# Neighbourhood probabilities of a two-layer encoder: the exchange of partition quarters as four writes to DRAM and one read back, instead of 16 transfers inside SBUF

## The chip, the cores and the metric

The kernel runs on one core of a Trainium2 chip. Its time is the device time of one execution, in microseconds (us). The core has a matrix engine (TensorE, PE), which reads SBUF and writes PSUM; a vector engine (VectorE, DVE); a scalar engine (ScalarE, ACT); a general engine (GpSimd, POOL); and a queue engine (SyncE, SP), which in this kernel issues the DMA transfers. SBUF has 128 partitions. A transfer is issued by SP and then moves on 16 DMA engines while SP goes on to its next instruction.

## The reference, cut to what matters

Two encoder layers on 512 tokens of width 1024, in float32. Each layer adds a mixer, a cross attention to 256 memory tokens and a convolutional feed-forward to x. Half of the mixer's heads (8 of 64 channels) do neighbourhood attention (NA): the tokens are a grid of 8 rows by 64 columns, and each query sees a window of 8 rows and 16 columns.

```python
scores = jnp.einsum('brqhd,brikhd->bhrqik', q, k_rows) * (dh ** -0.5)
scores = scores + bias[None]
scores = jnp.where(col_valid[None, None, None, :, None, :], scores, NEG_INF)
p = jax.nn.softmax(scores, axis=(-2, -1))
o = jnp.einsum('bhrqik,brikhd->brqhd', p, v_rows)
```

The change concerns p on its way from the softmax to the last product: scores come out with queries on partitions, and the product with V needs keys on partitions.

## The kernel before, in words

Every float32 operand of a matmul is split into a high and a low part, and three matmuls make one product. In the program's names, raw is a weight as it comes from DRAM, hi and lo its parts (made on ACT, L273, and POOL, L274), xg the normalised input, mm and sc tiles in PSUM, r and t tiles in SBUF, and u the tiles of this change: 128 partitions by 2048 elements, 1 MB, from a pool of two buffers.

The NA stage of a layer goes through the heads in four pairs p = 0 to 3, each in two units u = 2p + bp. Per pair:

- Scores (na_scores): eight 128x256 matmuls a unit, queries on partitions. DVE adds the bias and takes the row's bound (L766), ACT takes the exponential (L772). The K tile of a pair is split on ACT (L689) and DVE (L693) for one half of the partitions, and then "doubled": two DMAs copy it to the other half of the partitions (r<-r, 64 partitions, 256 KB each). The scores of the pair wait for that.
- Turn (na_turn): DVE takes the reciprocal of the sums (L782), ACT (L791) and POOL (L495) multiply, and DVE transposes 32x32 blocks into the pair's u tile (L793), eight instructions of 256 elements per unit.
- Exchange (na_exchange, L795 to L804): a block transpose leaves a block in the quarter of partitions (32 of them) in which it was. Sixteen DMAs move each quarter's four parts to the four quarters of a second u tile, 64 KB each, all issued by SP.
- Split (na_split): from that second tile, ACT casts the high part (L822, four instructions), and DVE and POOL subtract for the low part (L823, two each).
- Values (na_values): matmuls with V (mm<-r,r 128x256 on PE); two halves are added on ACT (L842) and DVE (L843, L844).

weave calls these steps, step s of the list working on unit s minus its lag; between them (None) the filler puts matmuls of projections, so that PE has work while a unit is on the other engines:

```python
weave(8, [(2, na_exchange), (3, na_split), None, (1, na_turn), (0, na_scores), None,
          (3, na_values_of), None], attn_fill.run, na_quanta)
```

The instructions of PE and of SP run in the order in which this code issues them. A doubling is issued by a rule of its own (late): its place comes when PE's programmed work has advanced far enough. The instructions of ACT, DVE and POOL are placed by a scheduler from the dependencies and from priorities, before the kernel runs, so a change at one place moves instructions near it. In every engine's program the order is then fixed: an instruction that waits holds up those behind it. An instruction that writes a buffer waits for the readers of what was in it.

Other transfers on SP that stand near the exchange: the weights (raw), the bias of the next pair (r<-in_bias), the memory tokens (r<-in_memT), the rope swaps of the other half of the heads (t<-t, four of 64 KB), a straddling of V (r<-r x5).

Of the kernel before, what the change touches and what calls it, by code (L numbers as in the profile page):

```python
# [10 lines left out]
F32 = mybir.dt.float32  # L11
# [8 lines left out]
S = 512  # L20
# [140 lines left out]
def weave(n, steps, filler, quanta):  # L161


    last = max(st[0] for st in steps if st)
    for s in range(n + last):
        pieces = iter(quanta(s))
        for st in steps:
            if st is None:
                filler(next(pieces))
            elif 0 <= s - st[0] < n:  # L170
                st[1](s - st[0])
# [3 lines left out]
def encoder_kernel(ctx: ExitStack, tc: tile.TileContext, t: dict, out: bass.AP):  # L175
    nc = tc.nc
    PE, SP = Counted(tc, nc.tensor), InOrder(tc, nc.sync)
    late = Late(PE)
    ACT_IN_ORDER = InOrder(tc, nc.scalar)
    ACT, DVE, POOL = Free(nc.scalar), Free(nc.vector), Free(nc.gpsimd)  # L180
# [6 lines left out]
    spool = ctx.enter_context(tc.tile_pool(name="spool", bufs=23))  # L187
    upool = ctx.enter_context(tc.tile_pool(name="upool", bufs=2))
    psum = ctx.enter_context(tc.tile_pool(name="psum", bufs=2, space=PSUM))

    @contextmanager
    def behind(n):
# [9 lines left out]
    def nm(s):  # L202
        uid[0] += 1
        return f"{s}_{uid[0]}"
# [18 lines left out]
    def turned():  # L223
        return upool.tile([P, 4 * S], F32, tag="u", name=nm("u"))
# [146 lines left out]
    for n in FIRST:  # L371
# [3 lines left out]
        u, k0, k1 = n  # L375
# [118 lines left out]
    def normalise(e, sums, col, eng=DVE):  # L494
        eng.tensor_scalar(e, e, sums[:, col : col + 1], 1.0, op0=ALU.mult, op1=ALU.mult)  # L495
# [89 lines left out]
    for n in FIRST:  # L585
# [3 lines left out]
        u, k0, k1 = n  # L589
# [6 lines left out]
        k = slice(k0, k1)  # L596
# [15 lines left out]
    for l in range(DEPTH):  # L612
# [163 lines left out]
        turns, flats = {}, {}  # L776

        def na_turn(u):

            p, bp = divmod(u, 2)  # L780
            es, sums = na.pop(u)
            DVE.reciprocal(sums, sums)  # L782
            if bp == 0:
                turns[p] = turned()
            to = turns[p].rearrange("p (k j b q) -> p j b k q", k=8, j=2, b=4)
            for j in range(2):
                for i in range(2):
                    if i or j:
                        normalise(es[j][:, i, :], sums, 2 * j + i, POOL)
                    else:  # L790
                        ACT.activation(es[j][:, i, :], es[j][:, i, :], AF.Copy, scale=sums[:, 2 * j + i : 2 * j + i + 1])  # L791
                for i in range(2):
                    DVE.transpose(to[:, j, 2 * bp + i], es[j][:, i, :].rearrange("p (k q) -> p k q", q=32))  # L793

        def exchange(src, chunks):  # L795

            dst = turned()
            to = dst.rearrange("p (r c n) -> p r c n", r=4, c=chunks)
            of = src.rearrange("p (c r n) -> p r c n", r=4, c=chunks)
            for d in range(4):  # L800
                for q in range(4):
                    r = (q + d) % 4
                    SP.dma_start(to[32 * r : 32 * r + 32, q], of[32 * q : 32 * q + 32, r])
            return dst  # L804

        def na_exchange(u):
            p, bp = divmod(u, 2)
            if bp == 1:
                flats[p] = exchange(turns.pop(p), 2)

        def na_split(u):
            p, bp = divmod(u, 2)
# [289 lines left out]
        def na_quanta(s):  # L1102
# [4 lines left out]
            if s == 3:  # L1107
# [2 lines left out]
                gqa_eps()  # L1110
            return [NA_FILL] * 3

        weave(8, [(2, na_exchange), (3, na_split), None, (1, na_turn), (0, na_scores), None, (3, na_values_of), None],
              attn_fill.run, na_quanta)
        weave(4 * NB, [(2, gqa_transpose_p), (1, gqa_normalise), (0, gqa_scores), (3, lambda u: gqa_values(u, 0)),
                       (4, lambda u: gqa_values(u, 1)), None], attn_fill.run, lambda s: [GQA_FILL[s]])
# [332 lines left out]
```

## Time and profile before

| | us |
|---|---|
| median of 3 runs | 1415.88 (1415.84 to 1417.39) |
| the profiled execution | 1421.33 |
| its span | 1419.6 |
| NA stage of layer 0 | about 55 to 165 |
| NA stage of layer 1 | about 755 to 865 |

The profile gives busy times of each engine in a stretch, the instructions of an engine in order of time with the idle time before each and what ended it (in square brackets), the waits grouped by what ended them, and the DMA's packets and bytes. A row "sc<-r,r x2 [4.61 <-DMA r<-r]" reads: two matmuls that make scores, before which the engine was idle for 4.61 us, until a DMA from a tile r to a tile r had landed. For SP (SPq) the length of a row is the time in which it issued the DMAs of the row, not the time that they took to land.

### The profile page before, as it was taken

Reading aid. Unit: us, or ns where it says so; the run is one execution under the profiler, and the core shown is the slowest. Engines: PE = TensorE matmul, PEld = TensorE weight load, DVE = VectorE, ACT = ScalarE, POOL = GpSimd, SP = SyncE. Lnnn points to the kernel's source line nnn. Section 1 sums busy time; section 2 is a strip of 40 time slices with the busy share of each in tenths; the row PEclk is TensorE's granted clock in tenths of the full one; section 3 lists DMA queues with packets and bytes.
Section 4 is the critical chain, followed back from the end, with each engine's and each line's share of the span. In section 5 each row is a group of like instructions: output and inputs, shape, how many; then the busy total and the mean of one; then the engine's idle time right before and its main releaser. Section 6 shows DMA issues by size and latency. Waiting matters only on the chain.

```text
span 1419.6 us, 19227 instructions
## 1 busy us (share of the span) xinstructions
PE 1359.4 (96%) x6940; PEld 1156.2 (81%) x6940; DVE 897.2 (63%) x1588; ACT 676.8 (48%) x1258; POOL 713.6 (50%) x509
## 2 busy tenths in 40 slices
PE   9987899999999999999997788999999999999997
PEld 7876789887888888888886777898888888888897
DVE  6667577557587178358546677765658852871874
ACT  6655467555444143234455546774644422342441
POOL 2556656554444444444544477476264444444441
PEclk9997899999999999999998999999999999999998
DMA  6774312231433332333257553123233333333331
GB/s 215 215 190 119 105 31 75 75 104 45 119 89 104 92 101 85 108 90 95 84 178 201 133 134 90 30 88 95 71 90 90 104 92 102 89 91 110 95 91 60
DMA packets 229598, 148.27 MB, mean 104 GB/s; under 512 B 8192, under 2 KB 222464, under 8 KB 229504
## 3 DMA queue, kind: packets, MB, share of 16 engines
q1 hardware_dynamic: 228400, 146.39, 35.6%
q8 instruction: 55, 0.90, 0.3%
q10 hardware_dynamic: 1104, 0.66, 0.1%
q14 instruction: 39, 0.32, 0.1%
HBM read 126.05 MB, written 2.10 MB: 90 GB/s over the span
## 4 chain that ended last, share of the span: by engine, by line
PE 81%; DVE 6%; DMA 4%; ACT 2%; SPq 2%; POOL 2%; issue 2%; ACTq 0%; DVEq 0%; POOLq 0%
PE mm L76 73%; PE sc L76 5%; PE tr L63 2%; SPq L63 2%; PE tr L76 1%; POOL lo L274 1%; DMA r<-in_memT 1%; DMA r<-r 1%; DMA raw<-in_w_in 1%; DVE u L793 1%; DVE r L823 1%; DMA r<-in_rope 1%; DVE r L709 1%; DVE mm L432 1%; ACT hi L273 1%
## 5 line engine op out<-in xcount | busy, mean ns | idle before, releaser
L274 POOL TENSOR_TENSOR lo<-raw,hi 128x1024 fp32r<-128x1024 f32 (+2 forms) x268 | 501.3, 1882 | 459.0 <-ACT hi L273 458.9
L76 PE MATMUL mm<-xg,hi 128*128 128x512 f32 x1920 | 602.3, 395 | 0.9 <-DVE t L844 0.9
L76 PEld LDWEIGHTS mm<-xg,hi 128*128 128x128 f32 x1920 | 362.7, 191 | 74.8 <-ACT t L842 1.1
L273 ACT CAST hi<-raw 128x512 fp32r<-128x512 f32 (+2 forms) x276 | 224.3, 836 | 338.8 <-PE mm L76 275.3
L76 PE MATMUL mm<-xg,lo 128*128 128x512 f32 x960 | 377.5, 393 | 0.0
L76 PE MATMUL mm<-r,hi 128*128 128x512 f32 (+1 forms) x1144 | 331.7, 374 | 1.9 <-DVE xg L446 1.6
L76 PEld LDWEIGHTS mm<-r,hi 128*128 128x128 f32 x1144 | 207.0, 189 | 40.1 <-DVE xg L446 3.2
L1272 DVE SCALAR_TENSOR_TENSOR t<-t,par,t 128x7 f32<-128x7 f32 (+1 forms) x352 | 201.9, 640 | 34.0 <-ACT t L1265 34.0
L76 PEld LDWEIGHTS mm<-xg,lo 128*128 128x128 f32 x960 | 182.9, 191 | 39.1
L76 PE MATMUL mm<-r,lo 128*128 128x512 f32 (+1 forms) x572 | 212.9, 372 | 0.0
L76 PEld LDWEIGHTS mm<-r,lo 128*128 128x128 f32 x572 | 107.8, 188 | 18.9
L495 POOL TENSOR_SCALAR t<-t,s 128x512 f32<-128x512 f32 (+1 forms) x112 | 66.9, 613 | 86.6 <-DVE s L782 43.9
L1257 DVE TENSOR_TENSOR t<-mm,rep 128x512 f32<-128x512 f32 x88 | 60.1, 687 | 77.7 <-PE mm L76 62.1
L76 PE MATMUL sc<-r,r 128*128 128x256 f32 (+1 forms) x352 | 76.7, 350 | 22.3 <-DMA r<-r 17.9
L1278 DVE TENSOR_TENSOR r<-t,r 128x512 fp32r<-128x512 f32 x44 | 90.5, 2057 | 7.4 <-ACT r L1277 4.3
L1274 ACT ACTIVATE t<-t 128x512 f32<-128x512 f32 x44 | 27.9, 633 | 134.8 <-DVE t L1272 134.7
L1301 DVE TENSOR_TENSOR xT<-xT,mm 128x512 f32<-128x512 f32 x32 | 21.9, 685 | 106.8 <-PE mm L76 106.8
L76 PE MATMUL mm<-r,r 128*128 128x256 f32 (+1 forms) x428 | 65.5, 304 | 18.0 <-DVE t L844 8.6
L76 PEld LDWEIGHTS sc<-r,r 128*128 128x128 f32 x352 | 54.7, 203 | 30.4 <-issue 10.4
L76 PEld LDWEIGHTS mm<-r,r 128*128 128x128 f32 x428 | 57.1, 194 | 23.0 <-issue 10.7
L1265 ACT ACTIVATE t<-t,par 128x512 f32<-128x512 f32 x88 | 66.8, 806 | 3.3 <-DVE t L1257 3.3
L959 ACT ACTIVATE t<-sc,s 128x512 f32<-128x512 f32 x64 | 44.1, 691 | 24.5 <-DVE s L957 21.7
(157 smaller groups left out, 1612.1 us busy)
## 6 DMA issues: line engine op xcount, KB each, us to landing
raw<-in_w_up SPq DMA_DIRECT2D x88, 512.0 KB, 3.6
raw<-in_w_in SPq DMA_DIRECT2D x33, 512.0 KB, 4.2
raw<-in_w_down SPq DMA_DIRECT2D x32, 448.0 KB, 3.4
u<-u SPq DMA_DIRECT2D x128, 64.0 KB, 2.0
raw<-in_w_mem_kv SPq DMA_DIRECT2D x16, 512.0 KB, 3.6
raw<-in_w_down SPq DMA_DIRECT2D x16, 512.0 KB, 3.6
r<-in_bias SPq DMA_DIRECT2D x16, 384.0 KB, 6.0
r<-r SPq DMA_DIRECT2D x22, 256.0 KB, 6.0
```

Of the source, the lines that this page charges most:

```text
L63: return lambda *a, **k: self.tc.keep_in_program_order(op(*a, **k))
L76: return self.tc.keep_in_program_order(self.engine.matmul(out, lhsT, rhs, **k))
L273: act.copy(hi[:, k], raw[:, k])
L274: (POOL if eng[0] == "P" else DVE).tensor_sub(lo[:, k], raw[:, k], f(hi)[:, k])
L495: eng.tensor_scalar(e, e, sums[:, col : col + 1], 1.0, op0=ALU.mult, op1=ALU.mult)
L959: ACT.activation(e, sc[j], AF.Exp, bias=nmx[:, c], accum_out=sums[:, c])
L1257: DVE.tensor_mul(u, us[side], ffn.rep)
L1265: ACT.activation(cc, u, AF.Identity, bias=par[:, l, CB + ch : CB + ch + 1], scale=w[1])
L1272: DVE.scalar_tensor_tensor(cc[:, dst], u[:, src], wi, cc[:, dst], op0=ALU.mult, op1=ALU.add)
L1274: ACT.activation(cs[0], cs[0], AF.Silu)
L1278: DVE.tensor_sub(acts[j][1], cs[0], f(acts[j][0]))
L1301: DVE.tensor_add(xT[m], xT[m], pm)
```

## The change

The 16 transfers from quarter to quarter become two steps. Four stores (na_store, one per source quarter, 32 partitions, 256 KB each) write a tile d in DRAM, whose layout puts the target's rows together. One load (na_load, 128 partitions, 1 MB) reads it into the second u tile. The load waits until the four stores have landed. It is a step of its own in the weave's list, ahead of the values and behind the scores, so other transfers can stand between the stores and the load. The transposes write the turned tile in another order (quarter outside, half inside), so that a store reads 2 KB runs; their number and size stay. A pool of two DRAM tiles is new. The lines behind the change move by one, and later by four: L822 and L823 become L826 and L827, L793 becomes L794.

```diff
+    dpool = ctx.enter_context(tc.tile_pool(name="dpool", bufs=2, space=bass.MemoryType.DRAM))
...
-            to = turns[p].rearrange("p (k j b q) -> p j b k q", k=8, j=2, b=4)
+            to = turns[p].rearrange("p (r c j b q) -> p j b c r q", r=4, c=2, j=2, b=4)
...
-                    DVE.transpose(to[:, j, 2 * bp + i], es[j][:, i, :].rearrange("p (k q) -> p k q", q=32))
-
-        def exchange(src, chunks):
-
-            dst = turned()
-            to = dst.rearrange("p (r c n) -> p r c n", r=4, c=chunks)
-            of = src.rearrange("p (c r n) -> p r c n", r=4, c=chunks)
-            for d in range(4):
-                for q in range(4):
-                    r = (q + d) % 4
-                    SP.dma_start(to[32 * r : 32 * r + 32, q], of[32 * q : 32 * q + 32, r])
-            return dst
-
-        def na_exchange(u):
+                    DVE.transpose(to[:, j, 2 * bp + i], es[j][:, i, :].rearrange("p (c r q) -> p c r q", c=2, r=4))
+
+        def store(src):
+
+            d = dpool.tile([4, 32, 4, S], F32, tag="d", name=nm("d"))
+            of = src.rearrange("p (r n) -> p r n", r=4)
+            for q in range(4):
+                SP.dma_start(d[:, :, q].rearrange("r k n -> k r n"), of[32 * q : 32 * q + 32])
+            return d
+
+        def na_store(u):
             p, bp = divmod(u, 2)
             if bp == 1:
-                flats[p] = exchange(turns.pop(p), 2)
+                turns[p] = store(turns.pop(p))
+
+        def na_load(u):
+            p, bp = divmod(u, 2)
+            if bp == 1:
+                flats[p] = turned()
+                SP.dma_start(flats[p], turns.pop(p).rearrange("r k q n -> (r k) (q n)"))
...
-        weave(8, [(2, na_exchange), (3, na_split), None, (1, na_turn), (0, na_scores), None, (3, na_values_of), None],
+        weave(8, [(2, na_store), (3, na_split), None, (1, na_turn), (0, na_scores), None, (2, na_load), (3, na_values_of), None],
```

PE's program is the same instruction for instruction. SP's differs at the eight pairs, and the scheduled engines differ in the two NA stages. Three places follow; a number behind a name tells tiles apart, and the same tile has another number in the two kernels.

The first is SP in layer 0, pair 0, before: the exchange, a weight, and the doubling of the next K tile (r_691, r_692).

```order
L63 DMA r_722<-in_rope 128x1024
L63 DMA u_726<-u_558 32x2x256 x16
L63 DMA raw_799<-in_w_in 128x8x128
L63 DMA r_691<-r_691 64x1024
L63 DMA r_692<-r_692 64x1024
L63 DMA r_859<-in_bias 128x768
```

And the same place now, where that doubling is of r_693 and r_694.

```order
L63 DMA r_724<-in_rope 128x1024
L63 DMA d_728<-u_560 32x4x512 x4
L63 DMA raw_789<-in_w_in 128x8x128
L63 DMA r_693<-r_693 64x1024
L63 DMA r_694<-r_694 64x1024
L63 DMA u_800<-d_728 128x2048
L63 DMA r_851<-in_bias 128x768
```

The doubling stands behind four stores instead of 16 transfers, and ahead of the load. In pair 0 of layer 1 the load stands ahead of the doubling.

The second place is DVE in layer 0, pair 1, before: the transposes of pair 2's first and second unit (u_1040 is the buffer that the exchange u_726<-u_558 has read, and L541 a normalisation of memory tokens), with the first subtraction of pair 1's split behind them.

```order
L541 SCALAR_TENSOR_TENSOR r_1116<-r_1002,par,r_1116 128x256 x2
L793 STREAM_TRANSPOSE u_1040<-t_875 128x8x32 x2
L793 STREAM_TRANSPOSE u_1040<-t_876 128x8x32 x2
L793 STREAM_TRANSPOSE u_1040<-t_1061 128x8x32
L793 STREAM_TRANSPOSE u_1040<-t_1062 128x8x32 x2
L793 STREAM_TRANSPOSE u_1040<-t_1061 128x8x32
L492 SCALAR_TENSOR_TENSOR r_902<-mm_1085,s_309,r_902 128x4x64
L766 ISA sc_1163,s_1173<-sc_1163,r_859 128x256
L766 ISA s_1173 128x1
L823 TENSOR_TENSOR r_1121<-u_1006,r_1121 128x512
```

Now the transposes of the first unit (from t_867 and t_868, the tiles that were t_875 and t_876) stand among the additions of pair 0's values.

```order
L493 SCALAR_TENSOR_TENSOR r_893<-mm_897,s_311,r_893 128x4x64
L847 TENSOR_TENSOR t_925<-mm_926,t_925 64x2x128
L794 STREAM_TRANSPOSE u_1020<-t_867 128x2x4x32
L847 TENSOR_TENSOR t_925<-mm_934,t_925 64x2x128
L794 STREAM_TRANSPOSE u_1020<-t_868 128x2x4x32
L848 TENSOR_TENSOR t_924<-mm_926,t_925 64x256
L794 STREAM_TRANSPOSE u_1020<-t_867 128x2x4x32
L794 STREAM_TRANSPOSE u_1020<-t_868 128x2x4x32
L847 TENSOR_TENSOR t_942<-mm_943,t_942 64x2x128
```

Half of pair 2's transposes moved ahead by the work of about one unit; the buffer they write is one that the load, and no longer the running exchange, shares with them.

The third place is layer 1, pair 1. On SP before, the doubling (r_6973, r_6974) stands behind the exchange, and the next exchange behind the straddling of V (r_7032, r_7033).

```order
L63 DMA u_7065<-u_6835 32x2x256 x16
L63 DMA r_6973<-r_6973 64x1024
L63 DMA r_6974<-r_6974 64x1024
L63 DMA raw_7254<-in_w_in 128x8x128
L63 DMA r_7032<-r_7030 64x1024
L63 DMA r_7032<-r_7030 64x512
L63 DMA r_7032<-r_7031 64x512
L63 DMA r_7033<-r_7031 64x512 x2
L63 DMA u_7320<-u_7099 32x2x256 x16
L63 DMA raw_7355<-in_w_in 128x8x128
L63 DMA t_7405<-t_7343 32x512 x4
```

And now, to the load of pair 2.

```order
L63 DMA d_7017<-u_6785 32x4x512 x4
L63 DMA r_6925<-r_6925 64x1024
L63 DMA r_6926<-r_6926 64x1024
L63 DMA u_7099<-d_7017 128x2048
L63 DMA raw_7196<-in_w_in 128x8x128
...
L63 DMA d_7262<-u_7039 32x4x512 x4
L63 DMA raw_7285<-in_w_in 128x8x128
L63 DMA t_7335<-t_7273 32x512 x4
L63 DMA u_7351<-d_7262 128x2048
```

The doubling went ahead of the load, and the load of pair 2 stands behind a rope swap (t_7335), ahead of which the whole exchange stood. On ACT at that place, before, the split of pair 1 stands ahead of the exponentials (L772) of the next unit.

```order
L273 CAST hi_7349<-raw_7028 128x512 x2
L822 CAST r_7178<-u_7065 128x512
L822 CAST r_7179<-u_7065 128x512
L822 CAST r_7180<-u_7065 128x512
L822 CAST r_7181<-u_7065 128x512
L772 ACTIVATE t_7238,s_7237<-sc_7226,s_7236 128x256 x2
L772 ACTIVATE t_7239,s_7237<-sc_7227,s_7236 128x256 x2
L791 ACTIVATE t_7238<-t_7238,s_7237 128x256
```

And now it stands behind them.

```order
L274 CAST hi_7279<-raw_6980 128x512 x2
L773 ACTIVATE t_7180,s_7179<-sc_7168,s_7178 128x256 x2
L773 ACTIVATE t_7181,s_7179<-sc_7169,s_7178 128x256 x2
L826 CAST r_7120<-u_7099 128x512
L826 CAST r_7121<-u_7099 128x512
L826 CAST r_7122<-u_7099 128x512
L826 CAST r_7123<-u_7099 128x512
L792 ACTIVATE t_7180<-t_7180,s_7179 128x256
```

The same goes for the subtractions on DVE and POOL there. In pair 2 of layer 1, POOL's second subtraction moved behind two operations of the rope (L917 and L922 before).

## The prediction

> **What bounds the kernel now.** I read the page first, then the stages as windows, then the waits of TensorE in the two stages that hold the change, then the order of time on SP, TensorE, VectorE and ScalarE there.
>
> ```profile
> span 1419.6 us, 19227 instructions
> PE 1359.4 (96%) x6940; PEld 1156.2 (81%) x6940; DVE 897.2 (63%) x1588; ACT 676.8 (48%) x1258; POOL 713.6 (50%) x509
> ```
> TensorE (PE) works 96% of the span: only its idle time, or a low clock, can be won. The windows show where those are (length, then busy time of PE, PEld, DVE, ACT, POOL, then granted clock, DMA share and GB/s):
>
> ```profile
> 55.00:165.00 110.00, 92.17 (x472) 78.97 (x471) 73.50 (x170) 59.36 (x145) 67.64 (x65) 0.86 0.59 160
> 165.00:755.00 590.00, 584.18 (x2899) 492.94 (x2898) 365.78 (x603) 277.00 (x478) 295.15 (x191) 1.00 0.32 93
> 755.00:865.00 110.00, 86.79 (x459) 74.34 (x458) 70.04 (x158) 56.70 (x139) 62.69 (x61) 0.89 0.56 150
> ```
> 55 to 165 is the neighbourhood stage (NA) of layer 0, 755 to 865 that of layer 1. PE idles 17.8 us (110 - 92.17) and 23.2 us (110 - 86.79) in them, at a clock of 0.86 and 0.89; in the 590 us between it idles 5.8 us at 1.00. The whole effect must come out of these 41 us and the low clock, or be added to them. The largest waits of PE there, layer 0 and then layer 1 (total, times, longest):
>
> ```profile
> PE sc L76 <- DMA r<-r: 5.3, 2, 4.6
> ...
> PE sc L76 <- DMA r<-r: 12.5, 4, 6.8
> ```
> The scores wait for the DMA that doubles K (r<-r). SP, which issues it, shows why (start, length, then a run of issues):
>
> ```profile
> 59.75 12.26 SPq L63 DMA_DIRECT2D u<-u  x16
> 72.75 1.19 SPq L63 DMA_DIRECT2D r<-r  x2
> 86.81 12.84 SPq L63 DMA_DIRECT2D u<-u  x16
> 753.69 12.55 SPq L63 DMA_DIRECT2D u<-u  x16
> 767.63 1.22 SPq L63 DMA_DIRECT2D r<-r  x2
> 786.67 12.70 SPq L63 DMA_DIRECT2D u<-u  x16
> 799.48 1.18 SPq L63 DMA_DIRECT2D r<-r  x2
> 811.71 11.29 SPq L63 DMA_DIRECT2D u<-u  x16
> 823.74 2.46 SPq L63 DMA_DIRECT2D t<-t  x4
> ```
> A pair's 16 transfers hold SP for 11 to 13 us, and three doublings stand behind them. VectorE had finished the K halves (L693) long before:
>
> ```profile
> 65.10 1.41 DVE L693 TENSOR_TENSOR r<-mm,r 64x512 fp32r<-64x512 f32 x2 [0.88 <-ACT r L689]
> 76.70 2.78 DVE L823 TENSOR_TENSOR r<-u,r 128x512 fp32r<-128x512 f32 x2
> 101.36 2.73 DVE L793 STREAM_TRANSPOSE u<-t 128x256 f32<-128x256 f32 x8 [2.41 <-DMA u<-u]
> 780.57 0.18 DVE L782 RECIPROCAL s<-s 128x4 f32<-128x4 f32 x1 [1.62 <-ACT t L772]
> 784.55 1.41 DVE L693 TENSOR_TENSOR r<-mm,r 64x512 fp32r<-64x512 f32 x2 [0.33 <-ACT r L689]
> ```
> K was there at 66.5 and 786.0, and the doublings left at 72.75 and 799.48. The third row is another cost: the next pair's transposes wait 2.41 us for the transfers to have read the buffer that they write. TensorE, with its waits in brackets:
>
> ```profile
> 78.02 0.77 PE L76 MATMUL sc<-r,r 128*128 128x256 f32 x2 [4.61 <-DMA r<-r]
> 80.92 0.41 PE L76 MATMUL mm<-hi,xg 128*128 128x256 f32 x1
> 85.36 2.09 PE L76 MATMUL mm<-r,r 128*128 128x256 f32 x16
> 88.13 0.28 PE L76 MATMUL mm<-lo,xg 128*128 128x256 f32 x1
> 106.28 1.20 PE L76 MATMUL mm<-r,r 128*128 128x256 f32 x8 [1.17 <-DVE r L823]
> 107.96 0.84 PE L76 MATMUL mm<-r,r 128*128 128x256 f32 x4 [0.49 <-DVE r L823]
> 111.25 1.22 PE L76 MATMUL mm<-r,r 128*128 128x256 f32 x4 [2.45 <-ACT t L901]
> 113.33 1.19 PE L76 MATMUL mm<-xg,hi 128*128 128x512 f32 x2 [0.85 <-DVE t L844]
> 774.32 0.77 PE L76 MATMUL sc<-r,r 128*128 128x256 f32 x2 [6.81 <-DMA r<-r]
> 776.04 1.62 PE L76 MATMUL sc<-r,r 128*128 128x256 f32 x6 [0.96 <-DMA r<-r]
> 803.10 0.77 PE L76 MATMUL sc<-r,r 128*128 128x256 f32 x2 [4.36 <-DMA r<-r]
> 804.29 1.62 PE L76 MATMUL sc<-r,r 128*128 128x256 f32 x6 [0.42 <-DMA r<-r]
> 809.60 1.60 PE L76 MATMUL mm<-r,r 128*128 128x256 f32 x12
> 829.03 1.21 PE L76 MATMUL mm<-r,r 128*128 128x256 f32 x8
> ```
> After a stall the clock is low: a 128x256 matmul shows 0.41 us at 80.92 and 0.28 us at 88.13. The 24 matmuls from 80.92 to 85.36 take 4.4 us; 24 at the pace of the later one (0.28, less the overlap that both share, so 4.4 x 0.28/0.41 = 3.0) would take 3.0. A stall of 4.6 us so costs about 1.4 more.
>
> **The change, part by part.** *Issues.* 128 transfers go, some 12 us of SP a pair. Four stores should hold SP as four t<-t do, 2.46 us; the read-back is one issue, 0.6 us at most (1.19/2). So a doubling behind the stores alone leaves 9.8 us earlier, and one behind the read-back leaves when the stores have landed.
>
> *The writes to DRAM and the read-back.* Before has no such operation. The bounds, from rows:
>
> ```profile
> q1 hardware_dynamic: 1497, 1.31, 44.3%
> DMA to landing us min/median/max: 2.0/2.0/7.2
> raw<-in_w_up SPq DMA_DIRECT2D x88, 512.0 KB, 3.6
> ```
> The first is the DMA from 135 to 148, where a pair's exchange is most of the traffic: 1.31 MB in 13 us x 0.443, so 0.227 MB/us from 32 partitions. The second is the landing of the 64 KB transfers. 1 MB in four 32-partition stores takes 1.05/0.227 = 4.6 us and about 2.0 us of landing: 6.6 us on an idle queue, and up to 5.2 more (7.2 - 2.0) behind a backlog. The low bound is the weights' pace, 3.6 us for 512 KB and so (3.6 - 2.0)/448 KB x 960 KB + 2.0 = 5.4 us for 1 MB; the high one is that a store to DRAM moves at half that of the exchange, 11.2 us. I take 6.6: the source, 32 partitions, is the same as in the first row. The read-back uses 128 partitions as the weights do: 5.4 us, between 4 and 9 (with the 5.2 of a backlog less what is shared).
>
> By the Trainium skill ("SBUF — State Buffer", Door 1) 32 partitions reach half of the ports and were measured at 189 GB/s for 1 MiB; that is below the 227 of the row here, and by it the stores would take 0.9 us longer and the sum come out some 3 us higher. The row decides.
>
> *Layer 0, pair 0: a gain.* K doubling leaves at about 66.5 rather than 72.75, the scores' stall (4.61 + 0.7) goes, and with it the slow clock: -5.3 - 1.4 = -6.7.
>
> *Layer 0, pair 0: a loss.* Stores start at 59.75 in the backlog that the 7.2 shows: 5.2 at most, I take 4; landed by 59.75 + 6.6 + 4 = 70.4; the read-back follows, landed at 75.8. The split starts then, and not at 73.50:
>
> ```profile
> 73.50 2.17 ACT L822 CAST r<-u 128x512 fp32r<-128x512 f32 x4 [1.01 <-DMA u<-u]
> ```
> From the first cast to the last subtraction (76.70 + 2.78 = 79.5) it takes 6.0 us, so it is ready at 81.8, and 0.5 later for transposes that now stand ahead of it on VectorE. PE, 6.7 us early, wants the values at 85.36 - 6.7 = 78.7: a new stall of 3.6, and 0.8 of low clock behind it: +4.4.
>
> *Layer 0, pair 1: a gain.* The transposes' 2.41 us wait goes, since the stores of the pair before are long over, and the read-back lands near 97 (stores from 86.81 less the 2.3 won so far, 84.5, to 91; load 5.4) before ScalarE's place for it. The four waits from 106.28 to 113.33, 1.17 + 0.49 + 2.45 + 0.85 = 5.0, hang on that late VectorE, and 1.0 of low clock: -6.0. Pairs 2 and 3 of this layer: the read-back lands about when the exchange did; nothing. Layer 0: -8.3.
>
> *Layer 1, pair 0.* The read-back stands ahead of the doubling. Stores from 753.69 land by 753.69 + 6.6 + 5 = 765.3; the doubling follows at 766.2 instead of 767.63, and if it lands as late after its issue, the 6.81 us stall shrinks by 1.4: -1.4.
>
> *Layer 1, pair 1: a gain.* The doubling stands behind the four stores alone: it leaves at about 787 instead of 799.48, and 4.36 + 0.42 go with 1.3 of clock: -6.1.
>
> *Layer 1, pair 1: a loss.* Its split now stands behind the next unit's softmax on ScalarE and VectorE; before, it stood ahead. In the rows above the reciprocal comes 780.57 - 777.66 (776.04 + 1.62) = 2.9 us after the last score. PE runs the scores from 803.10 - 7.5 = 795.6, ends at 796.9, the casts start near 800, and 5.5 us later all four parts are there: 805.5. PE wants them at 809.60 - 7.5 = 802.1: +3.4, and 0.4 of clock.
>
> *Layer 1, pair 2: a loss.* The read-back stands behind a rope swap (t<-t x4), and one of the split's POOL subtractions behind two rope operations. The stores leave when 811.71 less the 3.7 us won so far comes, 808; t<-t for 2.46, the load behind the landed stores (808 + 6.6 = 814.6), landed at 820 to 822; before, the last of the 16 (811.71 + 11.29 + 2.0) landed at 825.0, or 821.3 less 3.7. So no loss at the landing, but one on POOL, of the kind of
>
> ```profile
> 828.30 1.73 POOL L922 TENSOR_TENSOR t<-t,t 128x512 f32<-128x512 f32 x1
> ```
> Two such are up to 3.5 us, of which I take 3.0 for the values at 829.03: +3.0. Pair 3: its read-back, behind another rope swap, lands about when the exchange did; none. Layer 1: -1.4 - 6.1 + 3.8 + 3.0 = -0.7.
>
> *Transposes* keep count and size with another output stride; at 0.34 us each in the row at 101.36 (2.73/8), a third more would cost 7 us of VectorE in all, on an engine 63% busy: 0, at most +2.
>
> Sum: -8.3 - 0.7 = -9.0. The profiled execution took 1421.33 (1419.6 of span), 5.45 over the median of 1415.88; its sum gives 1412.3, and on the median 1406.9: **1407 us**.
>
> **The rivals.** *B, the losses don't come:* stores land as fast as the low bound, and the schedule's later places cost nothing, as PE has other work there. Without 4.4, 3.8 and 3.0 the sum is -20.2: 1396. For it speaks that the 41 us of idle could give it; against it, that the splits are visibly behind others in the new order. Chance 0.15.
>
> *C, gain and loss cancel:* the three losses are nearly doubled (+9), 1416: splits that are late once make the next unit late. A change within 0.2% (2.8 us) is about what can't be told from none. Chance 0.13.
>
> *D, slower:* one mechanism, a store to DRAM at the high bound, 11.2 us instead of 6.6. Each read-back lands 4.6 later. It shows where the split was late anyway (layer 0 pair 0, layer 1 pairs 1 and 2: +13.8), at the doublings behind stores or read-back (layer 0 pair 0 gets 2 of its stall back, layer 1 pair 0 3), and about 1 at pair 3 of layer 1: +20, 1427. It decides from 9.0/20 x 4.6 = 2.1 us more per pair, stores of 8.7 us. For it: no row shows a store's price. Against: the stores carry runs as long as the exchange's from the same partitions. Chance 0.27.
>
> The Trainium skill ("DMA: Bandwidth & Descriptors", Anatomy of one DMA) says that a transfer's signal waits for the receipt of its last byte and that this is heaviest for HBM; it gives about 2 us in all, which the 2.0 us here matches for SBUF. No row here shows it for DRAM, and it speaks for D.
>
> **How the numbers follow.** Forecast A, -9.0, has 0.45, its own range 1401 to 1413 (the losses of 11.2 half as large, or half as large again). Faster: A and B, 0.60; same: C, 0.13; slower: D, 0.27. The range reaches from just below B, 1394, to nearly D, 1425; outside lie the half of D that is dearer and a little of B.
>
> **What would show it.** Right: the profile after has no sc wait on r<-r in layer 0 and one of about 5 us, not 12, in layer 1; the transposes have no wait on DMA; the PE waits move to the values, on the split (L827), 3 to 4 us at each of three places; a store lands 3 to 6 us after its issue, the read-back 5. Wrong: stores of over 8 us, a read-back that lands after 77 in layer 0, or weights (raw) late behind SP's wait for the stores.

## The result, and the profile after

No difference that the measurement can tell: 1416.92 us (median of 20 runs, 1413.99 to 1421.20) against 1416.24 us before (median of 20, 1413.28 to 1419.95). The ratio is 1.0004, with a 95% interval of 0.9995 to 1.0013. I had forecast 1407, and given 0.13 to this case. The time lies inside my range of 1394 to 1425, but that range held nearly every case, so it says little. The profiled execution of the changed kernel took 1414.27 us, with a span of 1412.5.

The windows of the changed kernel answer to those of before (length, busy time of PE, PEld, DVE, ACT, POOL, clock, DMA share, GB/s):

```profile
55.00:165.00 110.00, 92.06 (x477) 78.38 (x475) 74.80 (x176) 61.65 (x151) 72.75 (x70) 0.89 0.66 197
165.00:755.00 590.00, 587.02 (x2923) 495.88 (x2924) 366.52 (x611) 277.44 (x483) 293.44 (x192) 1.00 0.33 97
755.00:865.00 110.00, 89.29 (x461) 75.65 (x460) 67.17 (x153) 57.36 (x139) 65.57 (x62) 0.88 0.56 170
```

In these fixed windows TensorE is idle about as before (17.9 and 20.7 us against 17.8 and 23.2). Between the marks that follow below, which hold the same matmuls in both kernels, it is 15.3 and 20.7 us against 17.8 and 23.2 in the same profile of before. But what it waits for has changed. The largest waits of PE in layer 0 and then in layer 1, after the change:

```profile
PE mm L76 <- ACT t L905: 3.6, 2, 2.9
PE mm L76 <- DVE t L848: 3.3, 4, 1.8
PE mm L76 <- DVE r L827: 2.8, 2, 1.8
...
PE sc L76 <- DMA r<-r: 0.7, 1, 0.7
```

```profile
PE mm L76 <- POOL r L827: 6.9, 3, 3.0
PE sc L76 <- DMA r<-r: 5.8, 4, 4.8
PE mm L76 <- DVE t L848: 3.5, 3, 1.9
```

The wait for the doubled K fell from 5.3 to 0.7 and from 12.5 to 5.8 us, as forecast; the transposes, which waited 6.3 us in all for the exchange before, now wait for no DMA; and waits for the split (L827) and for what hangs on the values took its place. On SP the four stores take 2 to 4 us, and the doubling of layer 1, pair 1 leaves 3.9 us after the start of the stores instead of 12.8:

```profile
57.81 2.98 SPq L63 DMA_DIRECT2D d<-u  x4
63.87 1.23 SPq L63 DMA_DIRECT2D r<-r  x2
65.30 0.42 SPq L63 DMA_DIRECT2D u<-d  x1
...
780.69 3.82 SPq L63 DMA_DIRECT2D d<-u  x4
784.61 2.07 SPq L63 DMA_DIRECT2D r<-r  x2
790.27 0.35 SPq L63 DMA_DIRECT2D u<-d  x1
```

The page's list of transfers has both new ones at the same median landing:

```profile
d<-u SPq DMA_DIRECT2D x32, 256.0 KB, 5.2
u<-d SPq DMA_DIRECT2D x8, 1024.0 KB, 5.2
```

To compare executions I use four marks that are the same instruction in every kernel: A, the group of eight 128x256 scores at 53.72 of the first profile; B, the first 128x512 scores of layer 0 (165.01); C, the last 128x256 score group of layer 1 ahead of the long stall (759.57); D, the first 128x512 scores of layer 1 (863.99). A to B and C to D hold what the change can reach in the two stages.

### The profile page after: what moved, and what is told of

The parts are those of the page before. It is cut to its first block, busy times and chain, and to the rows that moved or that the text cites. A ratio compares the mean times of both kernels' runs of the same rounds, so it can differ in the third digit from the quotient of the medians.

```text
span 1412.5 us, 19092 instructions
## 1 busy us (share of the span) xinstructions
PE 1358.0 (96%) x6940; PEld 1155.3 (82%) x6940; DVE 892.2 (63%) x1588; ACT 676.9 (48%) x1258; POOL 714.3 (51%) x509
## 4 chain that ended last, share of the span: by engine, by line
PE 83%; DVE 6%; DMA 4%; POOL 3%; ACT 2%; issue 2%; SPq 0%; DVEq 0%; POOLq 0%; ACTq 0%
PE mm L76 75%; PE sc L76 4%; PE tr L63 2%; POOL lo L275 1%; PE tr L76 1%; DMA r<-r 1%; DMA xT<-in_xT 1%; DVE r L710 1%; DMA t<-in_memT 1%; DVE u L794 1%; DMA u<-d 1%; DVE r L694 1%; DVE mm L433 1%; DVE xT L434 1%; SPq L63 0%
## 5 line engine op out<-in xcount | busy, mean ns | idle before, releaser
L76 PE MATMUL mm<-r,r 128*128 128x256 f32 (+1 forms) x428 | 70.3, 316 | 25.4 <-POOL r L827 7.6
L76 PEld LDWEIGHTS mm<-r,r 128*128 128x128 f32 x428 | 60.4, 204 | 31.8 <-POOL r L827 8.7
L76 PE MATMUL sc<-r,r 128*128 128x256 f32 (+1 forms) x352 | 73.2, 339 | 10.1 <-DMA r<-r 6.5
```

The lines of the kernel that those rows point to most:

```text
L76: return self.tc.keep_in_program_order(self.engine.matmul(out, lhsT, rhs, **k))
```

## The experiments

Each run was timed beside the kernel before, whose median in the three series of runs was 1417.33, 1416.14 and 1417.63 us; gains and losses below are worked out from the ratio to it.

### The two kernels, profiled again

No edit; first the kernel before, two more times.

> The kernel before, unchanged, for a second profiled execution. Theory N (the profile that the prediction read was an untypically slow execution, 5.1 us over the median of 1416.2): this execution comes out at 1414 to 1418, and the neighbourhood stage of layer 0 (from the second group of pair 0's scores, 53.72 in the first profile, to the first 128x512 scores of the other heads, 165.01: 111.3 us) is 2 to 5 us shorter, with smaller stalls at the doubled K than 5.3 and 12.5 us. Theory O (the stages are as the first profile shows them, and the change gives its gain back elsewhere): the stage of layer 0 takes 111.3 within 1 us, the stalls at the doubled K are 5.3 and 12.5 within 1, and the difference to the first profile lies outside the two stages.

> The kernel before, unchanged, a third profiled execution. The two neighbourhood stages, by the marks of the first two (from the second 128x256 score group before the exchange to the first 128x512 scores in layer 0; from the last score group before the stall to the first 128x512 scores in layer 1), took 111.3 + 104.4 = 215.7 us in the first and 108.0 + 103.4 = 211.4 in the second. If the first was untypical: 210 to 213. If both ends are as likely: 214 to 216.

The first profile of before, on which the prediction rests, from A to B and from C to D:

```profile
53.72:165.01 111.29, 93.45 (x482) 80.20 (x480) 74.28 (x172) 59.65 (x146) 68.88 (x68) 0.86 0.60 161
...
759.57:863.99 104.42, 81.21 (x435) 69.75 (x434) 66.73 (x149) 52.53 (x127) 60.44 (x58) 0.89 0.54 143
```

The second, an execution of 1417.08 us:

```profile
53.90:161.94 108.04, 90.37 (x481) 78.31 (x480) 73.01 (x172) 59.38 (x146) 68.36 (x68) 0.89 0.61 166
...
756.51:859.86 103.35, 83.32 (x436) 71.54 (x434) 66.74 (x149) 52.50 (x127) 61.62 (x58) 0.87 0.54 145
```

The third, an execution of 1419.46 us:

```profile
53.84:162.89 109.05, 91.58 (x482) 78.50 (x481) 73.51 (x172) 59.69 (x146) 68.91 (x68) 0.89 0.60 165
...
758.89:861.78 102.89, 81.84 (x435) 70.92 (x434) 65.84 (x149) 52.65 (x128) 61.37 (x58) 0.88 0.55 147
```

So the two stages took 215.7, 211.4 and 211.9 us with the same instructions, and the first profile is 4.0 above the mean of the other two (211.7). Theory N holds for the sum: layer 0 ran 2 to 3 us longer than in the others, layer 1 1.1 to 1.5. It doesn't hold for the stalls at the doubled K in layer 0, which were 5.7 and 5.4 in the later profiles against 5.3. What was longer there is TensorE's busy time for the same matmuls, 93.45 against 90.37 and 91.58 us, at a mean clock of 0.86 against 0.89. In layer 1 the stall at the doubled K of pair 1 was 4.36 in the first profile and 2.6 and 2.4 in the others. The third execution was slow outside the stages: from B to C it took 596.0 us, against 594.6 in the first two.

> The kernel after the change, unchanged, for a second profiled execution. In the first, layer 0's stage by the same two marks took 107.0 us and the whole 1414.27, 2.65 under its median of 1416.9. Theory N: an execution of 1416 to 1419, layer 0's stage 107 to 110. Theory O: layer 0's stage 107.0 within 1, and whatever is longer lies outside both stages.

The first of the changed kernel's two profiles:

```profile
52.79:159.81 107.02, 91.75 (x481) 79.16 (x480) 72.78 (x172) 59.61 (x147) 69.49 (x68) 0.89 0.69 206
...
753.07:856.92 103.85, 83.14 (x435) 71.06 (x434) 62.97 (x148) 52.75 (x128) 61.80 (x58) 0.87 0.61 185
```

The second, 1416.18 us, has 106.93 and 104.36: 210.9 and 211.3. So theory O holds for this kernel: the stages of its first profile were the usual ones. Against 211.7 the change moves the stages by half a us, which fits the ratio within its interval.

### The gain without the read-back's latency

The kernel before, with four transfers inside SBUF instead of 16:

```diff
-            for d in range(4):
-                for q in range(4):
-                    r = (q + d) % 4
-                    SP.dma_start(to[32 * r : 32 * r + 32, q], of[32 * q : 32 * q + 32, r])
+            for q in range(4):
+                SP.dma_start(dst[32 * q : 32 * q + 32], src[32 * q : 32 * q + 32])
```

> The kernel before, with the 16 transfers of a pair replaced by four of 256 KB inside SBUF, quarter to the same quarter: the quarters are not exchanged, so the values are computed from probabilities in the wrong place; bytes, matmuls and all other work are the same. SP is held as long as by the four stores, and there is no read-back. It prices the gain of the change without its latency. Theory G (the gains are what I summed: 6.7 and 6.0 in layer 0, 1.4 and 6.1 in layer 1): -20, so 1396 to 1399. Theory H (they are what the second profile of before shows against the profiles after: 5.0 and 3.4, 0.5 and 2.6, some of it made up by the next bound): -6 to -12, 1405 to 1411. Rival theory Z (the stage is bound elsewhere, by VectorE and ScalarE between units): less than 3.

1408.38 us, ratio 0.9946 (0.9934 to 0.9959): 7.6 us, theory H. So everything that I had counted as gain, 20.2 us, is worth 7.6 when nothing is lost to a read-back. Between this run and the changed kernel lie 8.2 us, by the two ratios, where I had 11.2 of losses. In the profile of the run with four transfers the first stage's waits of PE show where the rest went (the lines stand two earlier in this kernel, L842 for L844, L899 for L901):

```profile
PE mm L76 <- DVE t L842: 4.3, 4, 1.3
PE mm L76 <- ACT t L899: 3.7, 1, 3.7
PE mm L76 <- DVE r L693: 2.6, 2, 1.7
...
PE sc L76 <- DMA r<-r: 1.9, 2, 1.1
```

PE hardly waits for K (1.9 instead of 5.3 to 5.7) and waits for VectorE and ScalarE instead: for the second K split, for the additions of the values, for the rope. By this, the stall at K had been time in which those two caught up. In layer 1 a wait of 4.6 us at the doubled K is left, all of it in pair 0, whose doubling stands behind weights on SP; I had counted only 1.4 us of gain there.

### SP's hold on the doublings alone

The kernel before and the kernel after, with the doublings issued by ScalarE, and right behind the split of K instead of by the rule late; the edit is the same in both:

```diff
             def double():
-                for k, (r, o) in zip(kt, rows):
-                    SP.dma_start(f(k[o]), f(k[r]))
+                with behind(-300):
+                    for k, (r, o) in zip(kt, rows):
+                        ACT.dma_start(f(k[o]), f(k[r]))

             if not near:
-                late(2, double)
+                double()
```

> The kernel before, with the two DMAs that double K issued by ScalarE right after the split instead of by SP; the exchange stays as 16 transfers on SP. It takes away SP's hold on the doublings alone. If that hold is worth what I gave it (6.7 in layer 0, 1.4 and 6.1 in layer 1): -10 to -14, 1403 to 1407. If the doublings, once issued early, land late because they share the DMA engines with the exchange, or ScalarE's wait for VectorE's subtraction delays its other work: -5 to +2.

1413.43 us, ratio 0.9971 (0.9958 to 0.9983): 4.1 us, within the second expectation (5 faster to 2 slower) and under a third of the 14.2 that I had given these stalls. TensorE around pair 0 of layer 0 in this run, and then two rows of VectorE (the profiled execution, 1409.57 us, was the fastest of the seven):

```profile
76.79 1.23 PE L76 MATMUL mm<-r,r 128*128 128x256 f32 x8 [3.46 <-DVE r L824]
78.81 0.55 PE L76 MATMUL mm<-r,r 128*128 128x256 f32 x1 [0.79 <-DVE r L693]
79.81 1.86 PE L76 MATMUL mm<-r,r 128*128 128x256 f32 x7 [0.44 <-POOL r L824]
```

```profile
73.23 2.73 DVE L794 STREAM_TRANSPOSE u<-t 128x256 f32<-128x256 f32 x8 [0.99 <-DMA u<-u]
...
75.94 1.41 DVE L824 TENSOR_TENSOR r<-u,r 128x512 fp32r<-128x512 f32 x2
```

The scores wait for nothing, and PE is through the filler at 73.3. There it waits 3.46 and 0.44 us for the split and 0.79 for the split of the next K, 4.7 in all. VectorE's part of the split (75.94) stands behind the transposes, and these waited for the exchange until 73.23; ScalarE's cast ran at 73.70, right behind the exponentials, and did not wait for the exchange itself. So the stall at K had covered the time that the exchange and the work behind it need: one wait went and the other came to light.

> The kernel after, with the doublings issued by ScalarE in the same way. The stores and the read-back stay on SP in their order. After the change one doubling of layer 1 stands behind a read-back and shows a wait of 4.8 us; this takes it away. Expected -3 to -6 against after (1411 to 1414). If ScalarE's wait costs as much as it wins: within 2 us of after.

1411.30 us, ratio 0.9966 (0.9955 to 0.9977): 4.8 us under before and, by the two ratios, 5.4 under after, as expected (3 to 6). So the hold on the doublings that the change leaves on SP can be taken away with profit, though 3.3 of the 5.8 us of waiting at the doubled K in layer 1 remain in this run's profile (an execution of 1414.36 us, 3 over its median).

### The read-back's place

The kernel after, with the read-back one step earlier, and straight behind the stores:

```diff
-        weave(8, [(2, na_store), (3, na_split), None, (1, na_turn), (0, na_scores), None, (2, na_load), (3, na_values_of), None],
+        weave(8, [(2, na_store), (3, na_split), None, (2, na_load), (1, na_turn), (0, na_scores), None, (3, na_values_of), None],
...
-        weave(8, [(2, na_store), (3, na_split), None, (1, na_turn), (0, na_scores), None, (2, na_load), (3, na_values_of), None],
+        weave(8, [(2, na_store), (2, na_load), (3, na_split), None, (1, na_turn), (0, na_scores), None, (3, na_values_of), None],
```

> After the change, with the read-back one step earlier in the list (behind the first piece of filler, ahead of the turn), all else the same. In SP's program the read-backs of layer 1, pairs 2 and 3, then stand ahead of the rope swaps, the splits of layer 1, pairs 1 and 2, stand ahead of the next unit's softmax and of the rope operations again; in return the K doublings of layer 0 pair 0 and layer 1 pair 1 stand behind the read-back. If the late splits are what eats the gain (my losses of 3.4 to 3.8 and 3.0), values wait less by about 6 us in layer 1; if the doubling matters as much as I said, it costs some 5 us in layer 0 pair 0 and 5 in layer 1 pair 1, and the total is 0 to 5 us slower than the kernel after. If neither matters to the total, within 1 us.

1423.54 us, ratio to before 1.0045 (1.0029 to 1.0061), so some 6 us slower than after, just beyond the 0 to 5 that I had put. The split's waits are gone from the list of both stages, as expected, and the doubled K is back with what it cost:

```profile
PE mm L76 <- ACT t L905: 6.9, 2, 3.8
PE sc L76 <- DMA r<-r: 5.4, 2, 4.8
...
PE sc L76 <- DMA r<-r: 6.7, 3, 5.3
PE tr L76 <- ACT t L905: 5.4, 1, 5.4
```

The first two rows are of layer 0, the last two of layer 1; the last is a wait that no list of before or after has at this size. Layer 0's stage took 109.8 and layer 1's 107.5 us.

> After the change, with the read-back issued straight behind the four stores, all else the same: SP then stands still until the stores have landed, 5 to 8 us by the first profile, with weights and doublings behind it. Expected 2 to 8 us slower than the kernel after (1418 to 1425), most of it as stalls at the doubled K; like the run with the read-back one step earlier, within 1 us of it, if what stands behind the load on SP is not what bounds PE.

1419.30 us, ratio 1.0017 (1.0004 to 1.0029): about 2 us slower than after, at the low end. The scores behind the doubled K wait 6.2 us in layer 0 and 4.5 and 6.6 in layer 1, as expected; the profile names ScalarE and VectorE there, but these scores read nothing of the instructions that it names. It is not within 1 us of the other, and why the earlier place costs less than the middle one isn't settled: in layer 1 the two differ by 3.7 us (103.8 against 107.5), and on SP only by a weight that stands ahead of the read-back in pairs 0 and 2.

### The read-back's latency, shorter and longer

First I took the source of the read-back away: 1 MB of the input x instead of the tile that was stored.

```diff
-                SP.dma_start(flats[p], turns.pop(p).rearrange("r k q n -> (r k) (q n)"))
+                turns.pop(p)
+                SP.dma_start(flats[p], t["xT"].rearrange("(p a) n -> p (a n)", p=P)[:, 0 : 4 * S])
```

> The kernel after, with the read-back taking 1 MB of the input x from DRAM instead of the tile that the stores wrote: the values are computed from x and not from the probabilities; the stores are made as before, the read-back has the same size and place, but does not wait for them. It takes the wait for the stores away, and with it 3 to 8 us of a pair's latency. If the late splits eat the gain: 5 to 11 us faster than after (1406 to 1412), with the waits on the split (L827) gone from 2.8 and 8.7 us in the two layers to under 2 in all. If the order of the splits in the engines' programs, which this does not change, is what makes them late: within 3 us of after.

1416.58 us, ratio 0.9998 (0.9990 to 1.0007). This doesn't speak for the order of the splits, since the edit missed its aim: in layer 0 the read-backs of pairs 0 and 1 still left 8.8 and 8.5 us after the first store (7.5 and 8.2 in the kernel after). Pair 1 on SP, and the largest wait of SP there:

```profile
80.96 3.22 SPq L63 DMA_DIRECT2D d<-u  x4
89.41 0.36 SPq L63 DMA_DIRECT2D u<-in_xT  x1
...
SPq L63 <- DMA d<-u: 5.1, 1, 5.1
```

With two u buffers the read-back goes into the very buffer that the stores read, so it has to wait for them in any case. SBUF has no room for a third buffer. The next run shortened the stores instead, on top of that edit:

```diff
-                SP.dma_start(d[:, :, q].rearrange("r k n -> k r n"), of[32 * q : 32 * q + 32])
+                SP.dma_start(d[:, :, q, 0:P].rearrange("r k n -> k r n"), of[32 * q : 32 * q + 32, :, 0:P])
```

> The kernel after, with stores of a quarter of the bytes (64 KB each, the first 128 of 512 columns) and the read-back taken from the input x, 1 MB as before: the values are computed from x. The read-back still has to wait until the stores have read the buffer that it writes, but they end some 3 to 5 us earlier, and 0.75 MB less is moved a pair. Theory L (the read-back's latency is what eats the gain, at about 1 us of a pair's latency for 1 to 1.5 us in all over the exposed pairs): 4 to 7 us faster than after (1410 to 1413), with the two stages, 210.9 and 211.3 in the profiles of after, at 204 to 207. Rival M (what eats it is the order in which the splits stand in the engines' programs, and PE's own arrival at them): within 2 us of after.

1413.97 us, ratio 0.9975 (0.9965 to 0.9984): 3.5 us under before and, by the two ratios, 4.1 under after. The read-backs of the first seven pairs leave 6.8 us after the first store on average instead of 8.5 (the eighth stands behind a rope swap and leaves after 13.6 in both). Theory L, at the low end of its total; but the aim of 3 to 5 us was missed again, 1.7 came of it, and the profile's stages took 208.7 us, not 204 to 207. The run also moves 0.75 MB less a pair.

```diff
-            for q in range(4):
-                SP.dma_start(d[:, :, q].rearrange("r k n -> k r n"), of[32 * q : 32 * q + 32])
+            d2 = dpool.tile([4, 32, 4, S], F32, tag="d2", name=nm("d2"))
+            for e in (d2, d):
+                for q in range(4):
+                    SP.dma_start(e[:, :, q].rearrange("r k n -> k r n"), of[32 * q : 32 * q + 32])
```

> The kernel after, with four more stores of the same data to a second DRAM tile ahead of the four (nothing reads it): SP is held 2.5 us longer a pair, 1 MB more is written, and the read-back comes some 4 to 5 us later. By my rival D, 4.6 us more a pair cost 20 us: 1437. Theory L: 6 to 14 us slower than after (1423 to 1431), so that latency is paid for by half or less. Rival M: under 4 us slower.

1428.17 us, ratio 1.0067 (1.0053 to 1.0081): 8.9 us over after. The read-backs leave 11.8 us after the first store on average of the seven, 3.4 later. The total is in theory L's range, and rival M, which had under 2 us for the one run and under 4 for the other, fits neither: the stages do pay for latency, 2 to 3 us in all for one of a pair (4.1 for 1.7, and 8.9 for 3.4), where theory L had 1 to 1.5. The two runs also change how long SP and the DMA engines are held, so the price of latency alone is at most that. My rival D had 4.3 us for one (20 for 4.6).

### A version that beats both

The doublings on ScalarE and the read-back in the middle place:

> The kernel after, with the doublings issued by ScalarE (as in a_double_act, 4.8 us faster than before) and the read-back one step earlier (as in a_load_mid, which alone was some 6 us slower than after). With the doublings off SP nothing of the stage's K stands behind the read-back any more. If it was the doubling behind the read-back that made a_load_mid slow: 0 to 4 us faster than a_double_act (1407 to 1411). If it was the weights that stand behind it: 2 to 6 us slower than a_double_act.

1410.30 us, ratio 0.9939 (0.9923 to 0.9955), 8.6 us under before. So what made the middle place slow was the doubling behind the read-back. With it off SP the earlier read-back is worth having: the stages take 104.2 and 99.9 us, of which the first reads

```profile
53.78:157.98 104.20, 87.62 (x482) 76.12 (x480) 72.91 (x172) 59.59 (x146) 70.13 (x68) 0.93 0.69 212
```

Whether it beats the same kernel without the middle place (0.9966) by more than their intervals' width is less sure; the intervals just touch, and the two were timed in different series.

| kernel | ratio to before | 95% interval |
|---|---|---|
| after | 1.0004 | 0.9995 to 1.0013 |
| four transfers inside SBUF, no exchange | 0.9946 | 0.9934 to 0.9959 |
| before, doublings on ScalarE | 0.9971 | 0.9958 to 0.9983 |
| after, doublings on ScalarE | 0.9966 | 0.9955 to 0.9977 |
| after, read-back in the middle | 1.0045 | 1.0029 to 1.0061 |
| after, read-back at once | 1.0017 | 1.0004 to 1.0029 |
| after, read-back from the input | 0.9998 | 0.9990 to 1.0007 |
| after, short stores | 0.9975 | 0.9965 to 0.9984 |
| after, stores twice | 1.0067 | 1.0053 to 1.0081 |
| after, both edits | 0.9939 | 0.9923 to 0.9955 |

## Why the prediction was wrong

By its own marks I had forecast the two stages at 215.7 - 9.0 = 206.7 us. They take 211.1. Of the 9, some 4 were never there in the other two executions (215.7 against 211.7), and 4.4 are terms that came out otherwise than I had them. With both gone, some half a us is left of the 9.

Step by step, against the same profile of before, from the times since mark A or C (mark C stands at 753.07 after the change):

- *Layer 0, pair 0, gain of 6.7:* right. The last scores that waited for K start 25.8 us after A before (79.50) and 18.4 after (71.19): 7.4. Against the second profile it is 5.0, against the third 7.0.
- *Layer 0, pair 0, loss of 4.4:* about right, 5.0 measured (to the next score group: 92.77 - 79.50 before, 89.45 - 71.19 after). The waits at 76.83, 79.93 and 82.56 come to 1.82 + 1.18 + 0.58 = 3.6 us, just what I had; but only the first is on the split of the values, the others are on the split of the next K and on the additions, so the size is partly luck. The fillers run at a low clock until 87.3.
- *Layer 0, pair 1, gain of 6.0:* wrong, 3.5 us (from that score group to the end of pair 1's values: 113.33 - 92.77 before, 106.48 - 89.45 after). I had said that all four waits from 106.28 to 113.33 hang on the late transposes. The two on the split did and are gone; of the other two, 2.45 and 0.85, there remain 0.69 and 1.81, on the rope and the additions of the values.
- *Layer 0, pairs 2 and 3, nothing:* wrong, 1.7 lost (from there to mark B, 51.7 and 53.3). The read-backs of pairs 2 and 3 needed 7.7 and 8.8 us to land, not 5.4, and PE's waits there became 1.01, 0.76, 2.92, 0.16 and 0.45 (before 0.71, 1.26, 1.62 and 0.59).
- *Layer 1:* -1.4, -6.1, +3.8 and +3.0 forecast, -0.7 in all. Measured: -2.4, -3.6, +3.3 and +2.2, -0.6 in all (to the last scores that wait for K of each pair, 776.04 and 804.29 before, 767.17 and 791.80 after; then to the end of pair 1's values, 812.16 and 802.93; then to mark D). The sum is right by luck: the gain of pair 1 is 2.5 us short, pair 0's gain 1.0 larger and the two losses 1.3 smaller than I had them. In pair 1 PE's idle time fell by 4.0 us, near the 4.8 that I had from its two waits, but the 1.3 us of low clock did not come, for the mean clock in that stretch is 0.86 before and 0.87 after. And 4.36 us of that stall in the first profile are 2.4 to 2.6 in the others, so a usual execution has less to win.

Against the mean of the second and third profile of before, the same steps give gains of 6.0, 4.1, 1.4 and 2.4 us, 13.9 in all where I had 20.2, and losses of 5.8, 2.8, 2.3 and 2.2, 13.1 in all where I had 11.2. Layer 0 is then 1.5 us shorter (8.3 forecast) and layer 1 0.7 longer (0.7 shorter forecast).

The rows of before and then of after on TensorE that these steps rest on and that the prediction does not show:

```profile
92.77 1.12 PE L76 MATMUL sc<-r,r 128*128 128x256 f32 x8
...
812.16 0.72 PE L76 MATMUL mm<-r,r 128*128 128x256 f32 x4 [0.96 <-DVE t L844]
```

```profile
71.19 0.95 PE L76 MATMUL sc<-r,r 128*128 128x256 f32 x6 [0.74 <-DMA r<-r]
76.83 1.92 PE L76 MATMUL mm<-r,r 128*128 128x256 f32 x8 [1.82 <-DVE r L827]
...
89.45 1.12 PE L76 MATMUL sc<-r,r 128*128 128x256 f32 x8
...
103.92 0.74 PE L76 MATMUL mm<-r,r 128*128 128x256 f32 x4 [0.69 <-ACT t L905]
106.48 0.71 PE L76 MATMUL mm<-xg,hi 128*128 128x512 f32 x2 [1.81 <-DVE t L848]
...
130.01 1.23 PE L76 MATMUL mm<-r,r 128*128 128x256 f32 x4 [2.92 <-ACT t L905]
...
767.17 1.62 PE L76 MATMUL sc<-r,r 128*128 128x256 f32 x6 [0.65 <-DMA r<-r]
...
791.80 0.95 PE L76 MATMUL sc<-r,r 128*128 128x256 f32 x6 [0.18 <-DMA r<-r]
...
802.93 1.20 PE L76 MATMUL mm<-r,r 128*128 128x256 f32 x4 [1.02 <-DVE t L848]
```

The step that failed is thus the one that summed the gains: "the whole effect must come out of these 41 us" was right, but I took each wait of PE that SP caused as won in full. The run with four transfers says that of 20.2 us of such waits and their low clock, which is all that rival B hoped for, 7.6 can be had, and the run with the doublings on ScalarE that of 14.2 us 4.1 can. Behind a removed wait stood the next one, on VectorE, ScalarE or the exchange, that the stall had covered. I worked this out for pair 0 of layer 0 and for two pairs of layer 1, and not for the others. Nearly all the signs came that I had named for being right (0.7 us of stall at K left in layer 0 and 5.8 in layer 1, no wait of the transposes for a DMA, stores that land in 5.2 us); they show that the waits moved, and not what that is worth.

The other part is the base. The profiled execution was 5.45 us over the median, and I carried the difference of the sum to the median as if the stages were no longer than usual. They were, by 4: that execution, at 1421.33 us, lies above all 20 runs of before in the result (1419.95 at most).

Rival C had the right time but not the mechanism: I put it at losses nearly doubled, and they came out at 13.1 instead of 11.2; it was the gains that were short, by 6.3. Rival D's mechanism did not come: a store to DRAM is no dearer than I took it. In pair 0 of layer 0 they landed in 5.4 us (median), and the 256 KB transfers that stay inside SBUF, at the same place of the run with four, took longer. The DMA in that window of the changed kernel, and of the run with four transfers:

```profile
d<-u SPq DMA_DIRECT2D x4, 256.0 KB, 5.4
u<-d SPq DMA_DIRECT2D x1, 1024.0 KB, 8.4
```

```profile
u<-u SPq DMA_DIRECT2D x4, 256.0 KB, 7.8
```

What I had from the Trainium skill shows as little. Its page "DMA: Bandwidth & Descriptors" (Anatomy of one DMA), in a section on transfers that GpSimd issues, makes the receipt from HBM the heaviest. Here SP issues them, and on these busy queues a store to DRAM of the same size lands no later than one to SBUF, so nothing of that shows. By an estimate from the figure of the Trainium skill's page "SBUF — State Buffer" (Door 1) for 32 partitions, the stores would have taken 0.9 us longer than by the row, so 7.5 us instead of 6.6. In the five pairs of the changed kernel in which SP waited for the stores, the read-back left 8.2, 7.0, 6.9, 9.5 and 9.6 us after the first store, as late as by either or later, so these runs don't tell the two apart. In pair 0 of layer 0, where I had 10.6 with the backlog, it left after 7.5 us right behind the doubling, without a wait for the stores.

## What to carry to other kernels

A wait of TensorE is slack for the other engines. Before counting it as a gain, find for each the next operand that PE will ask for and when it is ready; the sum of the removed waits is only an upper bound, and here about a third of it could be had. Fewer transfers free the issuing queue, but a transfer that passes through DRAM in two dependent steps adds a latency, and what stood behind the old transfers now has to be placed against that latency: moving the transfer that blocked the scores to another engine's queue and then the read-back forward gave 8.6 us where the change alone gave none. And a profile that lies 5 us above the median of its own runs should be taken a second time, or its stage compared with another, before a term of 4 us is read from it.

## What the runs showed of the hardware that I had not expected

After waits of TensorE of less than 2 us, close together, the clock was low for longer than after one stall of 4.85 us. The changed kernel has the three waits of 1.82, 1.18 and 0.58 us at 76.83, 79.93 and 82.56, and a clock of 0.50 over 10 us; in the second profile of before, after the stall of 4.85 us that ended at 75.74, it was low over 7 us, and the 24 fillers that stand behind the same values ran at 1.00:

```profile
77.00:87.00 10.00, 8.24 (x37) 7.71 (x38) 7.83 (x17) 4.91 (x16) 3.43 (x5) 0.50 0.78 230
```

```profile
74.00:81.00 7.00, 4.44 (x20) 4.21 (x21) 6.42 (x16) 2.56 (x7) 4.06 (x3) 0.51 0.92 261
82.00:88.00 6.00, 5.53 (x46) 5.34 (x46) 3.91 (x10) 3.06 (x8) 1.39 (x4) 1.00 1.07 262
```

That the short waits made the stretch longer is not shown; after the like stalls of 4.61 and 4.74 us in the first and third profile of before the clock was low for about 7 and 3.5 us, so the length of one stall does not settle it either. The stage's mean clock is the same in these two profiles (0.89): the change moved the slow stretch, and did not remove it.

The time of one kernel in one place also varies more than I had thought. The same instructions of the same two stages took between 211.4 and 215.7 us in three executions (the second and third ran on different chips, and the record names none for the first, so it is open whether the chip or the execution makes it); the 16 issues of pair 0's exchange alone held SP for 12.26 us in the first and 10.98 in the second.
